# Vector products for the first two modulations: both weight tiles of a step loaded together, matmuls dealt to four column groups in turn

## The chip, the cores and the metric

The kernel runs on one core of a Trainium2 chip. The metric is device time in microseconds (us) of one launch. Before the change it is 1731.16 us, the median of three runs (1730.43 to 1734.97). A difference is given against that median.

## The reference, cut to what matters

One layer of a diffusion backbone, for 256 latent and 256 context tokens of width 2048, all in float32:

```python
mod_x = jnp.split(jax.nn.silu(c) @ w_ada + b_ada, 6, axis=-1)            # 6 rows of 2048
mod_c = jnp.split(jax.nn.silu(c_ctx)[None] @ w_ada + b_ada, 6, axis=-1)
qr, kr, vr, gr, cq, ckv, kpe = split_projection(modulate(x, mod_x[0], mod_x[1]) @ w_in)
qr_c, kr_c, vr_c, gr_c, cq_c, ckv_c, kpe_c = split_projection(modulate(ctx, mod_c[0], mod_c[1]) @ w_in)
# retention heads and latent attention heads over both streams, then
mix = jnp.concatenate([ret, from_heads(att)], -1) @ w_o
h = layer_norm(DEEPNORM_ALPHA * x + mod_x[2][:, None] * mix, ln1_w, ln1_b)
y = moe(modulate(h, mod_x[3], mod_x[4]))                                 # 32 gated experts, top 2
x_out = layer_norm(DEEPNORM_ALPHA * h + mod_x[5][:, None] * y, ln2_w, ln2_b)
```

`modulate` normalises a token and applies one shift (modulation 0) and one scale (modulation 1). These two have to be there before a block of `w_in` can be used; the change is in how they are computed.

## The kernel before

**Input projection in stages.** The first fifth of the kernel multiplies the modulated tokens with `w_in` (2048 x 4928). The contraction is cut into 16 blocks of 128, and these into six stages of 1, 1, 2, 4, 4 and 4 blocks (`STAGES`). Each stage goes over ten column blocks (nine of 512, one of 320). Five of them are for latent tokens alone, and five for context tokens too; all stages but the last take the five latent ones first. A stage loads its part of `w_in` in chunks of up to 1 MB: 3, 3, 5, 10, 10 and 10 chunks. A chunk is split into two float32r parts, a cast on ACT (L262, `whi`) and a subtraction on DVE (L263, `wlo`), and each product is three matmuls (L583 to L585): 24 for a full chunk of a latent column block, 48 with context. DVE adds the result to what earlier stages left (L592). A chunk's matmuls wait for `whi` and then for `wlo`.

**Vector products for modulations 0 and 1.** While stage s runs, shift and scale for the blocks of stage s+1 are made (`gemv_plan`, L503 to L530); those of the first stage are made at the start. Their weights (`ada01`) are tiles of 1 MB: one tile holds 16, 8 or 4 of the 16 contraction blocks, for one of the two modulations, at a width of 128, 256 or 512 columns. One matmul per contraction block k (L515) has 32 columns of weights (`csil`, two of them used) and writes 32 rows of one PSUM bank, the column group g = 2*m + k%2: tiles of shift use groups 0 and 1, tiles of scale groups 2 and 3. So a stage has 2, 4 or 8 tiles, each a `piece` of its own, in the order shift, scale, shift, scale. A last piece copies the bank on ACT (L521), adds up the groups with small matmuls (L524) and adds the bias on DVE (L526, `modc`). `modc` is used when tokens are transposed and modulated for the next stage (`xhat`; transposes L168, ACT L545, DVE L547). Rows of the trace count two records to a matmul of L515.

**Where the pieces stand.** After the matmuls of chunk ci the loop issues n = ceil(left / max(1, chunks - 2 - ci)) pieces. With ten chunks and nine pieces that is 2 after chunk 0 and 1 after each of the chunks 1 to 7.

**Loads.** All tiles of `w_in` and `ada01` go through `stream` (L141) into one pool `st` of four 1 MB buffers, on SP's queue, which issues in order and waits where the next buffer is not free. Rows of `w_ada` for modulations 2 to 5 (`ada25`) go through the same queue into a pool `sa` of two buffers; DVE uses them (L239, two instructions to a tile), some of them during the stages. The scheduler of the framework sets the order on each engine when the program is built; the queues then run in that order.

**After the projection** come retention, latent attention, output projection with the first norm, the router, the experts (382 loads of 1 MB) and the second norm.

## Time and profile before

| | us |
|---|---|
| median of three runs | 1731.16 |
| the three runs | 1730.43, 1731.16, 1734.97 |
| span of the profiled execution | 1728.5 |
| TensorE (PE) busy in it | 1595.0 (92%) |
| VectorE (DVE) busy | 860.4 (50%) |
| ScalarE (ACT) busy | 381.5 (22%) |

The profile gives no time for the profiled execution besides its span; the median of the runs lies 2.7 us above the span. PE is TensorE's matmuls, PEld its weight loads, SP the engine on whose queue the loads stand. In a row, `out<-in` are the names of the tiles that an instruction writes and reads (pG is the PSUM bank of the vector products, pA a bank of the projection, pT one for transposes), and what stands in square brackets is the engine's idle time before it, with what ended it.

### The profile page before, as it was taken

Reading aid. Unit: us, or ns where it says so; the run is one execution under the profiler, and the core shown is the slowest. Engines: PE = TensorE matmul, PEld = TensorE weight load, DVE = VectorE, ACT = ScalarE, POOL = GpSimd, SP = SyncE. Lnnn points to the kernel's source line nnn. Section 1 sums busy time; section 2 is a strip of 40 time slices with the busy share of each in tenths; the row PEclk is TensorE's granted clock in tenths of the full one; section 3 lists DMA queues with packets and bytes.
Section 4 is the critical chain, followed back from the end, with each engine's and each line's share of the span. In section 5 each row is a group of like instructions: output and inputs, shape, how many; then the busy total and the mean of one; then the engine's idle time right before and its main releaser. Section 6 shows DMA issues by size and latency. Waiting matters only on the chain. (4 is left out here: it accounts for less than half of the span.)

```text
span 1728.5 us, 21531 instructions
## 1 busy us (share of the span) xinstructions
PE 1595.0 (92%) x8730; PEld 958.4 (55%) x8730; DVE 860.4 (50%) x1563; ACT 381.5 (22%) x710; POOL 115.2 (7%) x94
## 2 busy tenths in 40 slices
PE   5999999987889899599999979999999999999995
PEld 4667686866868777344454434554444454444442
DVE  6877685798798777622331321332323233232306
ACT  3323232334665433410100000110010011001010
POOL 1000000074322100200000000000000000000001
PEclk8999999999999999799999999999999999999998
DMA  7787777756554589798999998999999999999981
GB/s 317 282 330 284 304 305 282 271 206 225 187 195 168 227 301 360 297 368 347 417 419 417 417 376 332 409 420 419 415 418 420 416 418 419 418 416 417 419 303 49
DMA packets 81591, 579.36 MB, mean 335 GB/s; under 512 B 9360, under 2 KB 9808, under 8 KB 11856
## 3 DMA queue, kind: packets, MB, share of 16 engines
q1 hardware_dynamic: 81360, 577.91, 83.8%
q8 instruction: 70, 1.15, 0.3%
q14 instruction: 33, 0.27, 0.0%
q0 software_dynamic: 128, 0.03, 0.0%
HBM read 575.81 MB, written 2.10 MB: 334 GB/s over the span
## 5 line engine op out<-in xcount | busy, mean ns | idle before, releaser
L1013 PE MATMUL pA<-st,xg 128*64 128x512 f32 x2032 | 447.5, 593 | 0.1
L1013 PEld LDWEIGHTS pA<-st,xg 128*64 128x64 f32 x2032 | 144.3, 137 | 273.0 <-issue 255.1
L1031 PE MATMUL pA<-st,hT 128*64 128x256 f32 x2048 | 238.5, 383 | 4.6 <-ACT hT L1022 4.6
L1017 DVE TENSOR_TENSOR hid<-pA,hid 128x256 f32<-128x256 f32 x32 | 13.6, 425 | 420.1 <-ACT hid L1016 420.1
L1031 PEld LDWEIGHTS pA<-st,hT 128*64 128x64 f32 x2048 | 140.0, 137 | 109.1 <-issue 26.9
L584 PE MATMUL pA<-wlo,xhi 128*128 128x512 f32 (+1 forms) x480 | 188.1, 392 | 10.3 <-DVE wlo L263 10.2
L583 PE MATMUL pA<-whi,xhi 128*128 128x512 f32 (+1 forms) x480 | 185.4, 394 | 3.4 <-ACT whi L262 3.3
L262 ACT CAST whi<-st 128x1024 fp32r<-128x1024 f32 (+3 forms) x130 | 124.7, 962 | 287.0 <-PE pA L585 175.0
L1035 DVE TENSOR_TENSOR Dm<-pA,ada_acc 64x256 f32<-64x256 f32 x256 | 108.1, 422 | 160.7 <-PE pA L1031 158.3
L585 PE MATMUL pA<-whi,xlo 128*128 128x512 f32 (+1 forms) x480 | 185.8, 387 | 0.0
L239 DVE SCALAR_TENSOR_TENSOR ada_acc<-st,c,ada_acc 128x1024 f32<-128x1024 f32 x128 | 176.8, 1401 | 11.2 <-DMA st<-in_ada_dram 11.0
L263 DVE TENSOR_TENSOR wlo<-st,whi 128x1024 fp32r<-128x1024 f32 (+2 forms) x122 | 134.7, 1112 | 56.0 <-ACT whi L262 55.4
L988 PEld LDWEIGHTS pT<-oh,nn 128*128 128x128 f32 x1024 | 125.6, 196 | 38.8 <-issue 38.0
L988 PE MATMUL pT<-oh,nn 128*128 128x128 f32 x1024 | 138.5, 286 | 7.1 <-PEq L1046 5.5
L994 ACT ACTIVATE xg<-pT,modt 128x128 f32<-128x128 f32 x128 | 58.4, 458 | 332.9 <-DVE xg L997 328.7
L1041 PE MATMUL pA<-Dm,sT 128*128 128x512 f32 x256 | 121.2, 596 | 4.9 <-DVE Dm L1035 4.9
L1016 ACT ACTIVATE hid<-pA 128x256 f32<-128x256 f32 x32 | 12.3, 384 | 497.2 <-PE pA L1013 497.2
L1042 DVE TENSOR_TENSOR h<-pA,h 128x512 f32<-128x512 f32 x128 | 88.3, 690 | 57.2 <-PE pA L1041 57.2
L583 PEld LDWEIGHTS pA<-whi,xhi 128*128 128x128 f32 x480 | 90.5, 191 | 37.6 <-ACT whi L262 17.9
L584 PEld LDWEIGHTS pA<-wlo,xhi 128*128 128x128 f32 x480 | 91.8, 191 | 32.2 <-DVE wlo L263 14.5
L585 PEld LDWEIGHTS pA<-whi,xlo 128*128 128x128 f32 x480 | 92.0, 192 | 16.3
L997 DVE TENSOR_SCALAR xg<-pT,modt 128x128 f32<-128x128 f32 x128 | 52.1, 408 | 50.8 <-PE pT L988 23.1
(342 smaller groups left out, 1462.2 us busy)
## 6 DMA issues: line engine op xcount, KB each, us to landing
st<-in_wexp_dram SPq DMA_DIRECT2D x382, 1024.0 KB, 12.3
st<-in_ada_dram SPq DMA_DIRECT2D x96, 1024.0 KB, 6.8
st<-in_win_dram SPq DMA_DIRECT2D x35, 1024.0 KB, 6.8
st<-in_wo_dram SPq DMA_DIRECT2D x16, 1024.0 KB, 5.0
st<-in_wuq_dram SPq DMA_DIRECT2D x3, 1024.0 KB, 4.8
xn<-in_x_dram SPq DMA_DIRECT2D x2, 1024.0 KB, 6.5
xn<-in_ctx_dram SPq DMA_DIRECT2D x2, 1024.0 KB, 17.0
st<-in_wukv_dram SPq DMA_DIRECT2D x2, 1024.0 KB, 5.0
```

Of the source, the lines that this page charges most:

```text
L239: V.scalar_tensor_tensor(accs[m][:, sl], w[:, sl], c2[:, k, 0:1], accs[m][:, sl], op0=OP.mult, op1=OP.add)
L262: A.copy(hi, src)
L263: (eng or V).tensor_tensor(lo, src, hi, op=OP.subtract)
L583: T.matmul(banks[t][:, :wd], xh[:, sl], hi[:, kk, :wd], start=fst, stop=False)
L584: T.matmul(banks[t][:, :wd], xh[:, sl], lo[:, kk, :wd], start=False, stop=False)
L585: T.matmul(banks[t][:, :wd], xl[:, sl], hi[:, kk, :wd], start=False, stop=lst)
L988: T.matmul(p[:, 128 * j:128 * j + width], nn[:, t, 128 * (k4 + j):128 * (k4 + j) + 128], oh[:, t, :width], start=(t == 0), stop=(t == 1))
L1013: T.matmul(pg[64 * cg:64 * cg + 64], xg[:, k, c0:c0 + 64], c[:, kk, 512 * cg:512 * cg + 512], start=(k == 0), stop=(k == KB - 1))
L1031: T.matmul(pd[64 * cg:64 * cg + 64, :256], hT[:, f % 2, 64 * (f // 2):64 * (f // 2) + 64], c[:, f, 256 * cg:256 * cg + 256], start=(f == 0 ...
L1035: V.tensor_tensor(Dm[rows, sl], pd[64 * cg:64 * cg + 64, :256], mod5[rows, sl], op=OP.mult)
L1041: T.matmul(p, sT[:K, t, :], Dm[:K, sl], start=True, stop=True)
L1042: V.tensor_tensor(h[:, t, sl], p, h[:, t, sl], op=OP.add)
```

## The change

A piece takes both tiles of a step j, of shift and of scale. They are loaded one directly behind the other, and the matmuls go over both: for each contraction block shift, then scale, so that the groups come in the order 0, 2, 1, 3. What is added into which group in which order is as before. A stage has 1, 2 or 4 such pieces and the last one, so with ten chunks and five pieces one comes after each of the chunks 0 to 3 and the last one after chunk 4. (The diff also takes out comments; from here on L515 is L517, L521 is L523, L524 is L526, L526 is L528, and L583 to L592 are one more.)

```diff
-        def piece(j, m):
+        def piece(j):
             def go():
                 if "p" not in box:
                     box["p"] = bank("G", 1)
                 p = box["p"]
-                c = stream(dram2(a["ada01"], base + (m * nch + j) * 128 * per * w, 128, per * w), per * w)
+                c = [stream(dram2(a["ada01"], base + (m * nch + j) * 128 * per * w, 128, per * w), per * w)
+                     for m in range(2)]
                 for kk in range(per):
                     k = j * per + kk
-                    g = 2 * m + (k % 2)
-                    T.matmul(p[32 * g:32 * g + 32, :w], csil[:, k], c[:, kk * w:kk * w + w],
-                             start=(k < 2), stop=(k >= KB - 2))
+                    for m in range(2):
+                        g = 2 * m + (k % 2)
+                        T.matmul(p[32 * g:32 * g + 32, :w], csil[:, k], c[m][:, kk * w:kk * w + w],
+                                 start=(k < 2), stop=(k >= KB - 2))
             return go
...
         for j in range(nch):
-            pieces.append(piece(j, 0))
-            pieces.append(piece(j, 1))
+            pieces.append(piece(j))
         return pieces + [last]
```

PE at the start, where shift and scale of the first block are made. `st_140` is the tile of shift, `xn_113` the normalised tokens. Before:

```order
L515 MATMUL pG_139<-st_140,csil_105 32x128 x16
L515 MATMUL pG_139<-st_158,csil_105 32x128 x16
L168 MATMUL pT_183<-ct_69,xn_113 128x128 x2
L524 MATMUL pG_178<-ct_69,row_176 128x4
L583 MATMUL pA_217<-whi_219,xhi_181 128x512
```

After (`st_142` is the tile of scale):

```order
L517 MATMUL pG_139<-st_140,csil_105 32x128
L168 MATMUL pT_183<-ct_69,xn_113 128x128 x2
L517 MATMUL pG_139<-st_142,csil_105 32x128
L517 MATMUL pG_139<-st_140,csil_105 32x128
L517 MATMUL pG_139<-st_142,csil_105 32x128
```

The two transposes of tokens stood behind all 32 products and now stand behind the first of them.

SP's queue in the stage of blocks 8 to 11, at its first chunks. `in_win` is `w_in`, `in_ada01` the weights of the vector products, `in_ada25` those of the later modulations. Before:

```order
L141 DMA st_1901<-in_win_dram 128x2048
L141 DMA st_2262<-in_ada25_dram 128x2048
L141 DMA st_1939<-in_ada01_dram 128x2048
L141 DMA st_2340<-in_ada25_dram 128x2048
L141 DMA st_1949<-in_win_dram 128x2048
L141 DMA st_1987<-in_ada01_dram 128x2048
L141 DMA st_1997<-in_win_dram 128x2048
L141 DMA st_2035<-in_ada01_dram 128x2048
L141 DMA st_2045<-in_win_dram 128x2048
L141 DMA st_2083<-in_ada01_dram 128x2048
```

After:

```order
L141 DMA st_1901<-in_win_dram 128x2048
L141 DMA st_2475<-in_ada25_dram 128x2048
L141 DMA st_1939<-in_ada01_dram 128x2048
L141 DMA st_2545<-in_ada25_dram 128x2048
L141 DMA st_1941<-in_ada01_dram 128x2048
L141 DMA st_1955<-in_win_dram 128x2048
L141 DMA st_1993<-in_ada01_dram 128x2048
L141 DMA st_1995<-in_ada01_dram 128x2048
L141 DMA st_2009<-in_win_dram 128x2048
L141 DMA st_2047<-in_ada01_dram 128x2048
L141 DMA st_2049<-in_ada01_dram 128x2048
L141 DMA st_2063<-in_win_dram 128x2048
```

Tiles of `w_in` and `ada01` alternated one to one; now two of `ada01` stand between two of `w_in`, and the four buffers of `st` go round in that order.

DVE at the end of the vector products in the stage of blocks 4 to 7. `modc` is the finished shift and scale, `wlo` the second part of the next tiles of `w_in`. Before:

```order
L592 TENSOR_TENSOR lv_95<-pA_1567,lv_95 128x512
L592 TENSOR_TENSOR cv_98<-pA_1568,cv_98 128x512
L592 TENSOR_TENSOR cv_98<-pA_1569,cv_98 128x512
L526 TENSOR_TENSOR modc_138<-pG_1632,bsel_108 128x16
L263 TENSOR_TENSOR wlo_1741<-st_1706,whi_1740 128x1024
L547 TENSOR_TENSOR xlo_1643<-xf_1647,xhi_1642 128x256
```

After:

```order
L263 TENSOR_TENSOR wlo_1333<-st_1328,whi_1332 128x1024
L263 TENSOR_TENSOR wlo_1349<-st_1328,whi_1348 128x1024
L592 TENSOR_TENSOR lg_96<-pA_1330,lg_96 128x512
L592 TENSOR_TENSOR lg_96<-pA_1331,lg_96 128x512
L528 TENSOR_TENSOR modc_138<-pG_1422,bsel_108 128x16
L263 TENSOR_TENSOR wlo_1387<-st_1382,whi_1386 128x1024
L263 TENSOR_TENSOR wlo_1403<-st_1382,whi_1402 128x1024
```

`modc` stood behind chunk 7, a context column block, and ahead of the split of the next chunk but one; it now stands behind chunk 3 (`lg`, a latent column block) and ahead of both splits of chunk 4 (`st_1382`), the chunk that PE takes next.

## Rows read from the trace of the kernel before

**Rows 1.** The head of the profile's page: the span, and the busy time of the engines.

```profile
span 1728.5 us, 21531 instructions
PE 1595.0 (92%) x8730; PEld 958.4 (55%) x8730; DVE 860.4 (50%) x1563; ACT 381.5 (22%) x710; POOL 115.2 (7%) x94
```

**Rows 2.** Busy time of the engines by stretch: the stretch, its length, busy time and instructions of PE, PEld, DVE, ACT and POOL, PE's granted clock as a share of full speed, the DMA engines' share, GB/s. The first two stretches are the stages of blocks 4 to 7 and 8 to 11, the others the last stage with retention and what follows it.

```profile
122.50:220.20 97.70, 97.70 (x446) 70.22 (x446) 67.53 (x82) 27.08 (x37) 0.00 (x0) 1.00 0.79 306
220.20:319.00 98.80, 98.80 (x482) 73.62 (x482) 68.12 (x81) 27.11 (x38) 2.30 (x2) 1.00 0.76 294
319.00:440.00 121.00, 106.17 (x512) 88.34 (x512) 108.03 (x169) 52.89 (x105) 53.08 (x49) 0.93 0.62 221
440.00:560.00 120.00, 108.24 (x624) 90.54 (x623) 104.02 (x195) 75.35 (x162) 32.46 (x18) 0.98 0.52 183
```

**Rows 3.** PE in order of time at three places of the 512 wide products: start in us, duration in us, engine, line, operation, tiles, shapes, records. The places are one matmul alone, one tile alone, and two tiles (of two pieces) with nothing between them.

```profile
146.42 1.05 PE L515 MATMUL pG<-st,csil 128*32 128x512 f32 x2
147.40 0.50 PE L584 MATMUL pA<-wlo,xhi 128*128 128x512 f32 x1
...
193.49 1.91 PE L515 MATMUL pG<-st,csil 128*32 128x512 f32 x8
195.33 0.50 PE L583 MATMUL pA<-whi,xhi 128*128 128x512 f32 x1
...
244.68 0.39 PE L584 MATMUL pA<-wlo,xhi 128*128 128x512 f32 x1
244.91 0.39 PE L585 MATMUL pA<-whi,xlo 128*128 128x512 f32 x1
245.23 1.94 PE L515 MATMUL pG<-st,csil 128*32 128x512 f32 x16
247.09 0.50 PE L583 MATMUL pA<-whi,xhi 128*128 128x512 f32 x1
247.43 0.40 PE L584 MATMUL pA<-wlo,xhi 128*128 128x512 f32 x1
```

**Rows 4.** The same view at the products 128 wide (first two rows) and 256 wide (next two), and at a run of three tiles 512 wide with the row behind it.

```profile
37.75 1.65 PE L515 MATMUL pG<-st,csil 128*32 128x128 f32 x22
...
47.26 1.97 PE L515 MATMUL pG<-st,csil 128*32 128x128 f32 x40
...
58.15 0.62 PE L515 MATMUL pG<-st,csil 128*32 128x256 f32 x2
...
65.06 1.92 PE L515 MATMUL pG<-st,csil 128*32 128x256 f32 x16
...
105.20 3.63 PE L515 MATMUL pG<-st,csil 128*32 128x512 f32 x24
109.58 0.73 PE L583 MATMUL pA<-whi,xhi 128*128 128x512 f32 x2 [0.75 <-ACT whi L262]
```

**Rows 5.** SP's queue from the second to the fifth stage: what a load waited for before it was issued, us in total, times, the longest in us.

```profile
SPq L141 <- PE pG L515: 146.4, 25, 10.9
```

**Rows 6.** Three loads issued one behind the other into an idle queue at 247.18, 247.60 and 248.07 us: tile, queue, number, size, us from issue to landing.

```profile
st<-in_win_dram SPq DMA_DIRECT2D x1, 1024.0 KB, 4.9
...
st<-in_ada_dram SPq DMA_DIRECT2D x1, 1024.0 KB, 7.0
...
st<-in_win_dram SPq DMA_DIRECT2D x1, 1024.0 KB, 9.0
```

**Rows 7.** Groups of instructions in 122.5 to 325 us, shapes kept apart: line, engine, operation, tiles, shapes, number, busy time in us, mean ns of one, idle time of the engine before them.

```profile
L239 DVE SCALAR_TENSOR_TENSOR ada_acc<-st,c,ada_acc 128x1024 f32<-128x1024 f32 x39 | 48.3, 1277 | 0.0
L263 DVE TENSOR_TENSOR wlo<-st,whi 128x1024 fp32r<-128x1024 f32 x37 | 44.8, 1221 | 25.6 <-ACT whi L262 25.3
L262 ACT CAST whi<-st 128x1024 fp32r<-128x1024 f32 x37 | 38.5, 1047 | 125.9 <-PE pA L585 109.8 <-DMA st<-in_win_dram 16.1
L521 ACT COPY row<-pG 128x512 f32<-128x512 f32 x2 | 1.2, 588 | 1.6 <-PE pG L515 1.6
```

**Rows 8.** PE and DVE in order of time at the end of the vector products in the stage of blocks 4 to 7.

```profile
219.38 0.95 PE L524 MATMUL pG<-ct,row 128*128 128x4 f32 x8
220.18 0.49 PE L583 MATMUL pA<-whi,xhi 128*128 128x512 f32 x1
220.36 0.17 DVE L526 TENSOR_TENSOR modc<-pG,bsel 128x16 f32<-128x16 f32 x1
220.65 1.23 DVE L263 TENSOR_TENSOR wlo<-st,whi 128x1024 fp32r<-128x1024 f32 x1
```

**Rows 9.** PE in order of time at the start of the kernel, and DVE in the same stretch.

```profile
12.52 5.72 PE L515 MATMUL pG<-st,csil 128*32 128x128 f32 x64 [12.52 <-DMA st<-in_ada_dram]
18.17 0.44 PE L168 MATMUL pT<-ct,xn 128*128 128x128 f32 x2
...
14.95 1.34 DVE L199 TENSOR_SCALAR xn<-xn,bnm,bnr 128x2048 f32<-128x2048 f32 x1
...
22.79 0.69 DVE L590 COPY lq<-pA 128x512 f32<-128x512 f32 x1 [0.71 <-PE pA L585]
23.39 2.46 DVE L194 BATCH_NORM_STATS2 bns<-xn 128x6 f32<-128x512 f32 x4
```

**Rows 10.** Two more stretches by engine, as in rows 2, in the first stage.

```profile
20.80:24.40 3.60, 3.50 (x8) 2.50 (x9) 2.89 (x5) 0.80 (x2) 0.00 (x0) 0.53 1.01 419
...
31.30:38.00 6.70, 5.79 (x17) 3.49 (x19) 4.66 (x9) 2.98 (x7) 0.00 (x0) 0.50 0.71 273
```

## The prediction

> **What bounds the kernel now.** I read the page's head first [rows 1]: PE is busy 92% of the span. Then the busy time by stretch [rows 2]: in the two stages of blocks 4 to 7 and 8 to 11 PE has no gap at all (97.70 of 97.70 us and 98.80 of 98.80), at a granted clock of 1.00 (2.4 GHz), while DVE is busy 69% of the time and the loads use 0.76 to 0.79 of the DMA engines. So a microsecond of vector products that goes shortens the projection by one, as long as no load or split becomes late; in the last stage and behind it DVE is nearly as full as PE (108.03 of 121 us, 104.02 of 120). Next I read PE in order of time at the vector products [rows 3, 4], to see what they cost in each form; then what SP's queue waits for [rows 5] and how long a load takes [rows 6], since the change doubles what a step needs; last the start [rows 9, 10], where PE waits anyway.
>
> The span is 1728.5 us and the median 2.7 us more; differences are worked out in the span and put on the median.
>
> **What the products save.** Taken from the start of one row to the start of the next [rows 3]: a matmul alone takes 147.40 - 146.42 = 0.98 us, four of one tile (two groups, in turn) 195.33 - 193.49 = 1.84 us, and eight of two tiles whose pieces stand side by side 247.09 - 245.23 = 1.86 us. Groups 0, 1 and then 2, 3 already run beside each other there, without the matmuls dealt in turn. So the new order gives nothing where two tiles already stood together; the gain is that all tiles now come in twos. The order of PE tells where each stands. A matmul that the scheduler puts alone in front still costs 0.98.
>
> - 512 wide, during blocks 2 and 3: before 0.98 + 0.98 + 1.85 + 1.84 + 4.38 (three tiles in a row, 109.58 - 105.20 in [rows 4]) + 1.87 = 11.9; now 0.98 + 1.85 + 1.87 and 3.72 for two pairs = 8.4. Saved 3.5.
> - During blocks 4 to 7: before 0.98 + 1.86 + 6 x 1.84 = 13.9; now 0.98 + 1.86 + 0.98 + 3 x 1.86 = 9.4. Saved 4.5. Three fewer changes between the two shapes: around the products at 245.23 the spacing of the projection's matmuls grows from 0.23 to 0.32 ahead and 0.34 behind [rows 3], so 0.2 each, 0.6. Together 5.1.
> - During blocks 8 to 11: before 1.86 + 6 x 1.84 = 12.9, now 1.86 + 0.98 + 1.86 + 2 x 1.86 = 8.4; with three changes of shape 5.1.
> - 256 wide: two tiles side by side 16 records in 1.85 (65.06), short blocks of one to two matmuls 0.55 (58.15) [rows 4]. Before ten blocks, 9.0 us with seven changes of shape more inside them, 10.3; now six short ones, one long and three such changes, 5.7. Saved 4.6.
> - 128 wide: two groups take 1.65 us for 22 records, 75 ns each [rows 4]; four 37.5. The 62 records of 37.75 and 47.26 cost 3.6 and then 62 x 0.0375 = 2.3. Saved 1.3.
>
> Sum 19.6. The pair does 8 x 0.98 = 7.84 us of lone matmuls in 1.86, 4.2 times as fast [rows 3]; I go by that. The Trainium skill speaks against it: "TensorE: Matmul & The Clock Gate", Part 3 (Packing small matmuls), measured 3.07 times for four packed, not four; the row disagrees.
>
> **What the loads cost.** SP waited 146.4 us for buffers that the products still held [rows 5]; before, that was hidden. The buffers of `st` go round: W0 a0 a0' W1, then a1 a1' W2 a2. a1' and W2 take the buffers of a0 and a0' and are issued when pair 0's products end; before, one tile of `ada01` stood between two of `w_in`, and each load had two steps to land. Loads issued one behind the other land 4.9, 7.0 and 9.0 us after their issue [rows 6]. From the end of pair 0 PE has 24 matmuls (5.71 us, 25 spacings of 0.23) and pair 1 (1.86), 7.57 us. W2, second in the queue and issued 0.4 later, lands at 7.4, its first part is cast in 1.05 [rows 7], so PE waits about 0.9. The whole stretch before the last pair has one such step in the 256 wide stage (1.0), 1.5 in the first 512 wide one (W1 there is behind pair 0 too), two in the next (1.6) and one in the last (0.8). Sum 4.9. Ends: 0 (the queue is not idle, but W2 may come before the gap that I assume), and with W2 third in the queue 9.0 + 0.4 + 1.05 - 7.57 = 2.9, and with `wlo` behind it (1.22) up to 3.5 a step.
>
> **What the end of the products costs.** Before, the small matmuls stood among those of a chunk already split (219.38, 220.18), and `modc` (220.36) had a split behind it that PE did not need at once [rows 8]. Now the last pair and the last piece stand behind one another on PE, and both splits of chunk 4, the next on PE, stand behind `modc` on DVE. After the last pair: copy of the bank 0.59 and its hand-over, 0.75; small matmuls 0.81 (220.18 - 219.38); `modc` 0.17; `wlo` 1.22: 2.95. Of that 0.81 was paid before, and some 0.2 runs beside whi's matmuls, so 1.9 a stage, for three stages 5.7. Ends: 0.7 (only the copy is waited for) and 2.2 each. No other work covers it: chunk 4 is next on PE, and the 24 matmuls before it are done.
>
> **The start.** 31 of the 32 products now stand behind two transposes that need the second token tile, ready at 14.95 + 1.34 = 16.29 [rows 9]. Before they ran from 12.52 to 18.17, 89 ns a record. Now 16.29 + 0.44 and 62 records at half of that, 2.8, end at 19.5, 1.3 later. On DVE one more copy (0.69) goes ahead of the context's statistics (23.39): 0.7. PE now stands idle up to 16.3, and I expect the stretches at 0.5 of the clock (1.2 GHz), which come after PE had worked little (20.80 to 24.40 and 31.30 to 38.00, [rows 10]), to take in some of the products; bound 0 and 2.8 (the products at half speed), I take 1.4. Sum 3.4; ends 2.0 and 62 x 0.089 + 0.44 + 16.29 - 18.17 + 0.7 = 4.8.
>
> Behind the projection nothing is moved that bears on the sum: the same tiles of `ada25` (two instructions of 1.28, [rows 7]) come before the end of the third 512 wide stage.
>
> **Sum.** -19.6 + 4.9 + 5.7 + 3.4 = -5.6: span 1722.9, median 1731.2 - 5.6 = 1725.6.
>
> **Rivals.**
> - B, the loads come in time. For it: the DMA engines have a quarter free in these stages [rows 2]. Against: the buffers set when a load starts, not the bandwidth. -19.6 + 5.7 + 3.4 = -10.5, 1720.7; with the split's wait at its lower end (3 x 0.7) 1717.
> - C, four groups give less in the new order than in the one place read: 1.86 was measured with the groups in the order 0, 1, 0, 1 and then 2, 3, 2, 3, not dealt in turn. A pair then lies between 1.86 and 2 x 1.84 = 3.68; at 2.5, 0.64 more for 12 pairs, it is 7.7: -5.6 + 7.7, 1733.3. Against: groups that are free of each other have no reason to care for the order. By the 3.07 of the Trainium skill's page "TensorE: Matmul & The Clock Gate", Part 3, a pair would take 7.84 / 3.07 = 2.55, near that value.
> - D, slower: W tiles land third. Its place is SP's queue: tiles of `ada25` stand between those of a step in the stage of blocks 8 to 11, and in a chunk of latent columns a step asks for 3 or 4 MB in 7.57 us where the third load lands at 9.0 [rows 6]. Then a step waits 3.5, five steps 17.5, and -19.6 + 17.5 + 5.7 + 3.4 = +7.0, 1738.2. It decides from 2.1 a step (19.6 - 5.7 - 3.4 = 10.5 in five steps). For it: nothing but the four buffers runs ahead. Against: two loads fit in a step, and before the `ada25` tiles came in the same places without a wait.
> - E, the gain isn't passed on: DVE, at 108.03 of 121 us in the last stage [rows 2], starts earlier but ends when it did, since SP's queue and its two `ada25` buffers feed it. 1731.
>
> **Chances.** The forecast (waits as summed, -5.6) 0.50, its own range 1720 to 1731; B 0.20, C 0.04, D 0.15, E 0.11. A measurement of this kernel can tell about 0.3%, 5.2 us, from no change. The forecast lies 0.4 beyond that bound: of its 0.50 I give 0.28 to faster, 0.21 to the same, 0.01 to slower; B gives 0.19 and 0.01; C 0.03 to the same and 0.01 to slower; D 0.04 to the same (where a step waits 2.1 to 2.9) and 0.11 to slower; E 0.01, 0.09 and 0.01. Faster 0.48, same 0.38, slower 0.14. The range of 8 in 10 leaves out the lower part of B and the upper half of D: 1715 to 1737.
>
> **What would show it.** Right: the pairs of eight 512 wide matmuls take 1.86 us each; PE has gaps of 0.8 to 1 us before `whi` of the third and fourth chunk of a stage, released by ACT, with the load landed about a microsecond before; a gap near 2 us behind the last pair, released by the copy and then by `wlo`; the first product of the projection starts 1 to 3 us after 20.80; the stage of blocks 4 to 7 is 1 to 2 us shorter than 97.7. Wrong on the loads: no gaps before `whi` (B), or gaps of 3 us and more with W third in the queue (D). Wrong on the groups: pairs of 2.5 us. Wrong on the passing on: the projection ends earlier by the sum, but the experts' loads begin no earlier (E).

## The result and the profile after

The changed kernel takes 1755.47 us (median of four runs, 1753.58 to 1755.84), the kernel before 1733.07 in the same comparison: a ratio of 1.0122, 95% interval 1.0105 to 1.0140. It is slower by 22 us, where 1725.6 us was forecast and the range ended at 1737. The spans of the two profiled executions are 1753.3 and 1728.5 us, 24.8 apart.

The head of the page after, which answers to [rows 1]:

```profile
span 1753.3 us, 21525 instructions
PE 1596.0 (91%) x8730; PEld 963.2 (55%) x8730; DVE 856.8 (49%) x1563; ACT 381.1 (22%) x710; POOL 111.8 (6%) x94
```

PE is busy as long as before, but that is not the same work. The matmuls of the vector products alone, over the first 420 us, before and after (busy time and records of PE and PEld, then PE's granted clock, the DMA engines' share, GB/s):

```profile
0.00:420.00 420.00, 58.98 (x384) 19.69 (x384) 0.97 0.74 284
```

```profile
0.00:420.00 420.00, 42.18 (x384) 12.90 (x384) 0.95 0.75 285
```

They are busy 16.8 us less. That PE's total doesn't fall goes with the clock: the mean granted clock of the span is 0.967 after and 0.979 before, and a matmul at half clock counts as busy for longer. PE's idle time grew by 23.8 us, from 133.5 to 157.3.

To see where, I took the same instruction in both traces as a mark: DVE's last addition of the 320 wide column block in each stage of the projection, the cast of the seventh `kn` tile (latent attention) and the last cast but one of `w_o` (output projection). That block is the last of a stage, except in the last stage, where it is the seventh of ten; so the stretch called latent attention begins with the last three chunks of the projection. The stretches of [rows 2] were cut elsewhere, at the end of a stage's vector products. Lengths from mark to mark in us, for the two kernels and for the experiments below:

| | start, block 0 | block 1 | 2, 3 | 4 to 7 | 8 to 11 | last stage, retention | latent attention | output projection |
|---|---|---|---|---|---|---|---|---|
| before | 54.05 | 36.04 | 53.41 | 96.74 | 98.82 | 126.71 | 87.17 | 127.68 |
| after | 55.46 | 32.93 | 61.01 | 97.10 | 102.38 | 132.86 | 91.75 | 129.04 |
| nodeal | 49.78 | 36.03 | 59.77 | 97.13 | 98.96 | 131.83 | 91.24 | 127.50 |
| oneload | 56.08 | 32.84 | 49.37 | 91.18 | 96.71 | 134.27 | 91.35 | 127.70 |
| startb | 49.16 | 33.47 | 61.99 | 97.24 | 100.01 | 131.46 | 92.17 | 127.60 |
| spread | 55.83 | 32.87 | 61.12 | 91.72 | 95.33 | 131.97 | 91.60 | 127.30 |
| eb2 | 54.36 | 32.79 | 61.07 | 96.88 | 98.47 | 132.42 | 91.41 | 127.53 |
| wahead | 53.98 | 32.95 | 61.80 | 99.16 | 100.64 | 133.40 | 91.97 | 127.48 |
| spread2eb | 50.27 | 32.99 | 57.67 | 90.98 | 95.33 | 131.22 | 93.74 | 128.00 |
| beb2 | 51.04 | 36.02 | 53.54 | 96.74 | 100.46 | 127.44 | 88.16 | 127.70 |
| eb4 | 55.57 | 33.01 | 61.34 | 97.28 | 102.93 | 131.09 | 92.49 | 127.54 |
| mix | 49.32 | 33.08 | 55.27 | 90.94 | 96.89 | 128.40 | 91.79 | 129.16 |
| mixav2 | 51.83 | 33.19 | 54.78 | 103.12 | 103.53 | 120.78 | 91.57 | 127.72 |
| aq | 53.73 | 32.78 | 60.59 | 97.02 | 98.37 | 129.85 | 95.04 | 128.84 |
| mixq | 52.30 | 32.91 | 54.84 | 90.93 | 95.29 | 130.82 | 96.33 | 129.26 |
| bq | 50.81 | 36.03 | 53.41 | 96.72 | 100.42 | 127.30 | 90.81 | 125.26 |
| a_noada | 57.00 | 32.93 | 61.99 | 96.29 | 98.39 | 107.22 | 79.19 | 125.63 |
| b_noada | 49.83 | 33.02 | 57.51 | 95.71 | 102.05 | 105.47 | 79.09 | 127.99 |

Some of these kernels run the same instructions in the same order up to a mark, and show how far one profile can be trusted. The start takes 50.8 to 54.1 in three profiles of before's order (before, beb2, bq) and 53.7 to 55.6 in four of after's (after, eb2, eb4, aq); the stage of blocks 8 to 11 takes 98.8 to 100.5 and 98.4 to 102.9. The other stages up to block 11 repeat within a microsecond. The last stage does not: with the same order on every engine it takes 132.9 in after and 129.9 in aq, and 128.4 in mix and 130.8 in mixq.

By the means of these three and four profiles the projection up to block 11 is 8.1 us longer after: +2.8, -3.2, +7.6, +0.3, +0.6. In the two profiled executions the last stage is 6.2 longer (4.4 by the means of before with bq and after with aq), latent attention 4.6, the output projection 1.4, and all that follows 2.9. The last two are near what profiles of one and the same code differ by.

**The five-chunk stage.** PE after, at the products made during blocks 2 and 3 (answers to the last row but one of [rows 4]):

```profile
100.31 0.73 PE L584 MATMUL pA<-whi,xhi 128*128 128x512 f32 x2 [1.73 <-ACT whi L262]
101.26 1.17 PE L584 MATMUL pA<-whi,xhi 128*128 128x512 f32 x2 [0.21 <-ACT whi L262]
...
108.08 4.61 PE L517 MATMUL pG<-st,csil 128*32 128x512 f32 x32
113.40 1.06 PE L526 MATMUL pG<-ct,row 128*128 128x4 f32 x8 [0.72 <-ACT row L523]
115.32 1.14 PE L168 MATMUL pT<-ct,xn 128*128 128x128 f32 x4 [0.86 <-ACT xf L546]
117.02 1.22 PE L584 MATMUL pA<-whi,xhi 128*128 128x512 f32 x2 [0.55 <-ACT whi L262]
```

From 108.08 on the two last pairs, the last piece and the transposes run with nothing of the projection among them: 8.9 us until the next matmul with `w_in` at 117.02. SP's queue there shows why (start, duration until the last of the group is issued, how many):

```profile
92.19 0.37 SPq L141 DMA_DIRECT2D st<-in_win_dram  x1
92.65 10.36 SPq L141 DMA_DIRECT2D st<-in_ada_dram  x4
110.04 3.49 SPq L141 DMA_DIRECT2D st<-in_win_dram  x4
```

A view prints `ada01` and `ada25` both as `in_ada`; the four of the second row are `ada01`. In this stage the loop puts two pairs after chunk 0 and two after chunk 1. The four `ada01` tiles of two pairs fill the four buffers. Behind chunk 1 the next tile of `w_in` is issued only at 110.04, when the first of the two pairs is done; it lands 4.8 later, and its cast makes PE wait to 117.02. The two pairs after chunk 0 delay the tile issued at 92.19 in the same way, and PE waits 1.73 for its cast (100.31).

**The clock.** The same three stretches before and after (columns as in [rows 2]), before first:

```profile
86.00:94.00 8.00, 8.00 (x40) 3.87 (x39) 7.74 (x13) 2.94 (x5) 0.00 (x0) 1.00 0.50 189
100.00:106.00 6.00, 6.00 (x32) 4.32 (x34) 3.52 (x5) 0.00 (x0) 0.00 (x0) 1.00 0.95 358
114.00:122.00 8.00, 8.00 (x46) 5.31 (x45) 5.15 (x7) 2.68 (x3) 0.00 (x0) 1.00 0.88 360
```

```profile
86.00:94.00 8.00, 7.22 (x35) 3.56 (x34) 7.03 (x11) 1.58 (x2) 0.00 (x0) 1.00 0.54 197
100.00:106.00 6.00, 5.47 (x16) 4.05 (x17) 3.15 (x4) 1.21 (x2) 0.00 (x0) 0.72 0.97 386
114.00:122.00 8.00, 6.58 (x21) 4.68 (x21) 4.27 (x8) 5.35 (x10) 0.00 (x0) 0.57 0.94 393
```

In before's profile the clock is 1.00 in every 2 us from 86 to 340. After, it falls to 0.5 (1.2 GHz) behind the wait that ends at 100.31, again behind those at 112 to 117, and for a few us near 170, 264 and 290. PE counts as busy in such a stretch and does half the work. Not every fall has a wait before it: near 264 PE had not waited for anything since 188, and in beb2 and bq, which run before's order, the clock falls near 256 with PE busy all the time. This is beb2:

```profile
256.00:259.40 3.40, 3.40 (x11) 2.73 (x10) 0.00 (x0) 0.00 (x0) 1.83 (x2) 0.50 0.91 321
```

What such a stretch costs depends on what sets the pace. In eb2 and aq, with after's order, the clock stays at 1.00 behind the wait that ends at 100.31 after, and the whole stage of blocks 2 and 3 is no shorter (after, eb2, aq; the clock is the last column but two):

```profile
88.39:149.40 61.01, 56.24 (x264) 39.57 (x264) 40.15 (x57) 17.37 (x28) 0.00 (x0) 0.92 0.74 282
```

```profile
87.14:148.22 61.08, 54.06 (x264) 37.60 (x264) 40.16 (x57) 17.38 (x28) 0.00 (x0) 0.97 0.76 286
```

```profile
86.51:147.10 60.59, 53.94 (x263) 37.59 (x264) 40.14 (x56) 17.20 (x28) 0.00 (x0) 0.97 0.78 288
```

PE's busy time falls by 2 us there and its waits grow by as much (in eb2 it waits 1.45 at 110.05 for an `ada01` tile to land): the loads set the pace. In the stage of blocks 8 to 11 it is otherwise. There the clock stays at 1.00 in eb2 and aq, which take 98.5 and 98.4 us; it is 0.95 in after and eb4, which take 102.4 and 102.9.

**The two ten-chunk stages.** The waits in the stage of blocks 4 to 7 after, at a late tile of `w_in` and at the end of the products:

```profile
167.36 0.73 PE L584 MATMUL pA<-whi,xhi 128*128 128x512 f32 x2 [1.09 <-ACT whi L262]
168.62 0.50 PE L585 MATMUL pA<-wlo,xhi 128*128 128x512 f32 x1 [0.53 <-DVE wlo L263]
...
185.66 1.06 PE L526 MATMUL pG<-ct,row 128*128 128x4 f32 x8 [0.73 <-ACT row L523]
186.61 0.73 PE L584 MATMUL pA<-whi,xhi 128*128 128x512 f32 x2
188.12 0.50 PE L585 MATMUL pA<-wlo,xhi 128*128 128x512 f32 x1 [0.78 <-DVE wlo L263]
```

That is 1.6 for the loads and 1.5 for the end. The stage of blocks 8 to 11 has the same four waits (0.94, 0.53, 0.73 and 0.78).

**The products themselves** came out as forecast: two tiles 512 wide take 177.30 - 175.45 = 1.85 us, and the 62 records 128 wide now 50.71 - 48.83 = 1.88, less than the 2.3 us of the prediction.

```profile
48.83 1.95 PE L517 MATMUL pG<-st,csil 128*32 128x128 f32 x62
50.71 0.50 PE L584 MATMUL pA<-whi,xhi 128*128 128x512 f32 x1
...
175.45 1.92 PE L517 MATMUL pG<-st,csil 128*32 128x512 f32 x16
177.30 0.74 PE L584 MATMUL pA<-whi,xhi 128*128 128x512 f32 x2
```

### The profile page after: what moved, and what is told of

The parts are those of the page before. It is cut to its first block, busy times and chain, and to the rows that moved or that the text cites. A ratio compares the mean times of both kernels' runs of the same rounds, so it can differ in the third digit from the quotient of the medians.

```text
span 1753.3 us, 21525 instructions
## 1 busy us (share of the span) xinstructions
PE 1596.0 (91%) x8730; PEld 963.2 (55%) x8730; DVE 856.8 (49%) x1563; ACT 381.1 (22%) x710; POOL 111.8 (6%) x94
## 5 line engine op out<-in xcount | busy, mean ns | idle before, releaser
L584 PE MATMUL pA<-whi,xhi 128*128 128x512 f32 (+1 forms) x480 | 185.7, 399 | 17.0 <-ACT whi L262 16.8
L1036 DVE TENSOR_TENSOR Dm<-pA,ada_acc 64x256 f32<-64x256 f32 x256 | 108.1, 422 | 160.6 <-PE pA L1032 158.3
L239 DVE SCALAR_TENSOR_TENSOR ada_acc<-st,c,ada_acc 128x1024 f32<-128x1024 f32 x128 | 176.6, 1400 | 14.6 <-DMA st<-in_ada_dram 14.5
L586 PEld LDWEIGHTS pA<-whi,xlo 128*128 128x128 f32 x480 | 93.2, 194 | 16.8 <-DVE xlo L548 0.2
```

The costliest lines, as they stand in the source:

```text
L239: V.scalar_tensor_tensor(accs[m][:, sl], w[:, sl], c2[:, k, 0:1], accs[m][:, sl], op0=OP.mult, op1=OP.add)
L584: T.matmul(banks[t][:, :wd], xh[:, sl], hi[:, kk, :wd], start=fst, stop=False)
L586: T.matmul(banks[t][:, :wd], xl[:, sl], hi[:, kk, :wd], start=False, stop=lst)
L1036: V.tensor_tensor(Dm[rows, sl], pd[64 * cg:64 * cg + 64, :256], mod5[rows, sl], op=OP.mult)
```

## The experiments

Theories first: Q, tiles of `w_in` come late because `ada01` tiles stand before them in a queue with four buffers, and the clock falls after each wait; F, the dealt groups themselves cost; S, the start; and for what lies behind block 11, where no line was changed: O, the engines' order, which the scheduler works out anew for the whole program; P, DVE with its `ada25` work. Each kernel's time is one run unless an interval is given.

**nodeal.** The pairs without the dealing: shift's tile, then scale's.

```diff
-                for kk in range(per):
-                    k = j * per + kk
-                    for m in range(2):
+                for m in range(2):
+                    for kk in range(per):
+                        k = j * per + kk
```

> As the changed kernel, but a pair's eight matmuls run over the tile of shift first and then over that of scale, not dealt in turn. Marks are the end of the stage of blocks 8 to 11 (the last context column block added by DVE): 339.1 us before, 348.9 after. Theory Q (the tiles of w_in come late behind two ada01 tiles, and PE's clock falls after each wait): the order of the matmuls means nothing, a pair of 512 wide takes 1.9 us here too, and the mark lies at 347 to 351. Rival F (dealing to four groups itself costs): the pairs are quicker or the waits go, and the mark lies at 343 or below.

1742.9 us. The mark lies at 341.7, so by the bar set F wins. But the bar tells little: after's own order gives 342.5 to 350.1 (after, eb2, eb4, aq). By stage F does not win: the stages of blocks 2 to 7 are nearly as after (59.8, 97.1). The gain is at the start (49.8 against 55.5), where the products now run in before's order, and the stage of block 1 loses the saving again (36.0 against 32.9). There the scheduler scatters the small products into the same ten blocks as before, and only dealt ones find all four groups; at 512 wide a pair takes 1.87 us (171.63 to 173.50) undealt too.

**oneload.** A pair loads one tile and uses it twice.

```diff
-                     for m in range(2)]
+                     for m in range(1 if si else 2)]
+                c = (c + c)[:2]
```

> As the changed kernel, but from the second stage on a pair loads the tile of shift alone and uses it for scale too (the scale is wrong; 15 loads of 1 MB are left out). The same matmuls in the same places. Theory Q: with one ada01 tile to a step the next tile of w_in comes in time, the waits of the stage of blocks 2 and 3 (about 8 us) and of the two after it go, the granted clock is 1.00 from 122 to 319 us, and the end of the stage of blocks 8 to 11 lies at 328 to 334 (339.1 before, 348.9 after). Rival F (the four groups, or the end of the products behind modc, cost): the mark stays at 345 or above.

1732.2 us. The stages of blocks 2 to 11 take 49.4, 91.2 and 96.7, at a clock of 1.00 and with no gap in the first two (49.40 of 49.40 us busy, 91.18 of 91.20); in the third the clock is at 0.50 from 279.4 to 286.2, which theory Q had not expected. The mark lies at 326.2, below the 328 to 334 expected. So the saving is there, 4.0 and 5.6 us against before in the first two stages (3.5 and 5.1 forecast; 1.3 of the 4.0 were gaps before), and in the changed kernel the second load takes it and more. F falls.

**startb.** The start alone as before (a piece is told which tiles to take).

```diff
         for j in range(nch):
-            pieces.append(piece(j))
+            if si == 0:
+                pieces.append(piece(j, (0,)))
+                pieces.append(piece(j, (1,)))
+            else:
+                pieces.append(piece(j))
```

> As the changed kernel, but at the start the tiles of shift and scale are taken one after the other as before. Theory Q: only the start moves: the first cast of w_in at 20.1 as before (21.9 after), and the end of the stage of blocks 8 to 11 1 to 2 us earlier than after, 347 to 348. Rival S (the start delays the loads of the context and shifts the whole queue): more than 4 us of the 9.8 go.

1746.0 us. The first stage ends 6.3 us earlier than after, and the mark lies at 341.9, 7.0 earlier: by the bar set rival S, against the expectation. Against all four profiles of after's order (342.5 to 350.1) it is 0.6 to 8.3, so the size is not settled. PE at the start, after and then in this run:

```profile
12.38 0.60 PE L517 MATMUL pG<-st,csil 128*32 128x128 f32 x2 [12.38 <-DMA st<-in_ada_dram]
13.40 0.48 PE L168 MATMUL pT<-ct,xn 128*128 128x128 f32 x1 [0.42 <-DVE xn L199]
16.21 0.48 PE L168 MATMUL pT<-ct,xn 128*128 128x128 f32 x1 [2.33 <-DVE xn L199]
16.62 3.30 PE L517 MATMUL pG<-st,csil 128*32 128x128 f32 x62
20.32 0.39 PE L526 MATMUL pG<-ct,row 128*128 128x4 f32 x2 [0.41 <-ACT row L523]
```

```profile
12.29 4.75 PE L517 MATMUL pG<-st,csil 128*32 128x128 f32 x64 [12.29 <-DMA st<-in_ada_dram]
16.97 0.44 PE L168 MATMUL pT<-ct,xn 128*128 128x128 f32 x2
17.41 0.39 PE L526 MATMUL pG<-ct,row 128*128 128x4 f32 x2
19.60 0.50 PE L588 MATMUL pA<-whi,xhi 128*128 128x512 f32 x1 [1.81 <-ACT whi L262]
```

The transposes ahead of the products hold PE to 16.62, as forecast from [rows 9], and the first matmul with `w_in` comes at 22.51 against 19.60: 2.9. The rest goes with the clock, which in this run is 1.00 throughout the first stage, and 0.63 from 31.3 to 38 us after.

**spread.** Pairs after chunks 0, 2, 4 and 6 in the ten-chunk stages.

```diff
+            if nchunk == 10 and todo:
+                n = 1 if ci in (0, 2, 4, 6, 7) else 0
```

> As the changed kernel, but in the ten-chunk stages the pairs come after chunks 0, 2, 4 and 6 and the last piece after chunk 7. Theory Q: each pair's loads have two steps again, so the stages of blocks 4 to 7 and 8 to 11 take 93 to 95 us each at a clock of 1.00 (96.7 and 98.8 before, 97.1 and 102.4 after), while the stage of blocks 2 and 3 stays at 60 to 62 (53.4 before, 61.0 after). Rival F: those stages stay at 97 or more. Theory O for what comes behind (the scheduler's order on ACT in the last stage, not the lateness): the stretch from the end of the stage of blocks 8 to 11 to the last split of the output projection, 341.6 before and 353.7 after, follows the order of ACT there; rival P (lateness carried on by loads): it falls back to about 342 as the lateness goes.

1740.3 us. 91.7 and 95.3 in the two stages, 61.1 in the one that was not spread: theory Q, the first even below its 93 to 95, and 5.0 and 3.5 us under before. What follows block 11 stays long (132.0 and 91.6) though this kernel is 2 us ahead of before at that mark, so lateness is not handed on.

**eb2, eb4.** The second decay table in two and in four buffers.

```diff
-        Eb = rt.tile([128, 384], F32, name="Eb", bufs=1)
+        Eb = rt.tile([128, 384], F32, name="Eb", bufs=2)
```

In the last stage PE waited 8.9 us for a cast on ACT after, and ACT for POOL:

```profile
390.82 0.80 PE L584 MATMUL pA<-whi,xhi 128*128 128x512 f32 x1 [8.91 <-ACT whi L262]
392.07 0.80 PE L585 MATMUL pA<-wlo,xhi 128*128 128x512 f32 x1 [0.46 <-DVE wlo L263]
```

```profile
388.42 0.61 ACT L350 ACTIVATE Eb<-rfb,r_lg 128x384 f32<-128x384 f32 x1 [8.61 <-POOL Dt L351]
388.94 0.89 ACT L355 ACTIVATE xq<-rfb,r_lg 128x256 f32<-128x256 f32 x2
389.74 1.03 ACT L262 CAST whi<-st 128x1024 fp32r<-128x1024 f32 x1
```

> As the changed kernel, but the second decay table of a retention head (Eb, L350 on ACT, used by POOL at L351) has two buffers in place of one. Up to the end of the stage of blocks 8 to 11 nothing is changed (mark at 348 to 350). Theory O (in the last stage the scheduler now puts the second head's Eb on ACT ahead of the cast of a w_in tile, and that Eb waits for POOL): PE's wait of 8.9 us for that cast goes, and the stretch from that mark to the last addition of the 320 wide column block falls from 132.9 to 125 to 128 us (126.7 before). Rival P (POOL and DVE are simply full there, so another wait takes its place): it stays at 131 or more.

> As the changed kernel, with Eb in four buffers (in the run with two, the third head's Eb stood ahead of the next cast and waited for POOL in the same way). Theory O: with no Eb waiting, ACT's casts of the last stage come in time, and the stretch from the end of the stage of blocks 8 to 11 to the last addition of the 320 wide block falls from 132 to 125 to 128 us. Rival P (DVE, with three more ada25 instructions of 1.3 to 1.8 us in the stretch than before, 39 against 36, and POOL beside it are the bound): another wait of the same size takes its place and it stays at 131 or more.

1747.1 and 1753.9 us. The wait for the cast goes, and DVE takes its place: with four buffers PE has this row there,

```profile
387.89 0.80 PE L585 MATMUL pA<-wlo,xhi 128*128 128x512 f32 x1 [4.02 <-DVE wlo L263]
```

and the stretch is 132.4 and 131.1, within the 129.9 to 132.9 of after's own order. The longest wait of a view was not the cause; O falls for ACT, P stands.

**wahead.** The next chunk's tile of `w_in` is loaded ahead of the pair's two.

```diff
+            if si >= 2 and n and ci + 1 < nchunk:
+                nw = sum(NBW[m] for m in chunks[ci + 1])
+                ahead[ci + 1] = stream(dram2(a["win"], off, 128, nk * nw), nk * nw)
             for f in todo[:n]:
```

> As the changed kernel, but from the third stage on the next chunk's tile of w_in is loaded ahead of a pair's two tiles, not behind them. Theory Q (the tile of w_in is late because it stands behind ada01 tiles in a queue of four buffers): the stages of blocks 2 and 3, 4 to 7 and 8 to 11 take 54 to 57, 92 to 95 and 95 to 98 us (61.0, 97.1 and 102.4 after). Rival L (a step simply asks for more than the loads bring, whatever the order): the waits move to the products, and the stages stay within 2 us of after.

1754.2 us; 61.8, 99.2 and 100.6: rival L. The order in the queue is not the point. I read it as three tiles a step in four buffers, whichever stands first: fewer tiles a step (oneload) and more steps (spread) help. A pool with more buffers was not run.

**spread2eb and beb2.** The first puts startb, spread and eb2 together, with one pair after each of the chunks 0 and 1, two after chunk 2 and the last piece after chunk 3 of the five-chunk stage; the second is before with eb2's line.

```diff
+            if nchunk == 5 and todo:
+                n = (1, 1, 2, 1, 0)[ci]
```

> The pairs and the dealt matmuls, with the start as before, the pairs after every second chunk in the ten-chunk stages, after chunks 0, 1, 2 (two) and 3 in the five-chunk stage, and Eb in two buffers. Theory Q with S and O: the stages take 49, 33, 52 to 56, 91 to 93 and 95 to 97, the last stage's stretch 125 to 128 as in the run with Eb alone, and the total is 1720 to 1729, 2 to 11 us below before. Rival: the stage of blocks 2 and 3 keeps its waits (62), and the total stays within 3 us of before or above it.

> The kernel before with Eb in two buffers, nothing else. Theory O: before, the cast stood ahead of the waiting Eb, so there is little to gain: the stretch from the end of the stage of blocks 8 to 11 to the last addition of the 320 wide block is 122 to 127 us (126.7), the total 1727 to 1734. Rival: Eb's single buffer cost before as well, 5 us or more, and the total falls below 1727.

1733.08 us, ratio 1.0010 (0.9995 to 1.0025), and 1732.14, ratio 0.9999 (0.9989 to 1.0009): no difference that can be measured in either. For the first the rival holds: 57.7 in the stage of blocks 2 and 3 where 52 to 56 was expected, 131.2 behind it where 125 to 128 was, and no gain in the total. It is 11.8 us ahead of before at the end of block 11 (327.2) and has given nearly all of it back by the end of latent attention (131.2 and 93.7). That left what lies behind as the question.

**mix and mixav2.** The start and the products of the five-chunk stage singly, the others in pairs, spread in the ten-chunk stages. mixav2 adds Eb's four buffers and moves `ada25` tiles forward in the program:

```diff
-ADA_V = [[0] * 10, [0] * 10, [0] * 5, [1] * 10, [1] * 10, [2] * 4 + [1] * 6]
+ADA_V = [[0] * 10, [0] * 10, [1] * 5, [1] * 5 + [2] * 5, [1] * 5 + [2] * 5, [1] * 10]
```

> Pairs dealt to four groups only where two steps lie between them: the start and the products made during the five-chunk stage are taken singly as before, those of the 128 and 256 wide stages in pairs, those of the two ten-chunk stages in pairs after chunks 0, 2, 4 and 6. Theory Q: stages of 49 to 51, 33, 53 to 54, 91 to 92 and 95 to 96, so the stage of blocks 8 to 11 ends at 321 to 326 us (339.1 before). The rest decides the total: if the stretches behind follow the engines' order, which is nearer to before's here (88 ada25 instructions on DVE up to the last addition against 94 after and 86 before), 126 to 129 and 87 to 89 and a total of 1715 to 1721; if pairs as such make them longer, 131 to 133 and 91 to 93 and 1723 to 1729.

> The run before this one, with Eb in four buffers, and with more of the ada25 tiles put into the stages of blocks 2 to 11 (5, 15 and 15 in place of 0, 10 and 10) and fewer into the last stage: 70 of DVE's 128 ada25 instructions stand ahead of the end of the stage of blocks 8 to 11 (50 before), 32 in the stretch behind (36 before, 39 after). If DVE's ada25 instructions bound that stretch (rival P), it falls to 124 to 128, for 7 fewer of 1.3 to 1.8 us than after; the stages of blocks 2 to 11 grow by 0 to 6 us in all, since their DVE has room (69% busy before) but their loads less. If not, it stays at 131. The total 1714 to 1728.

mix: 1729.78 us, ratio 0.9984 (0.9967 to 1.0001), the lowest median, and just not told from before; latent attention takes 91.8 where the better case was to bring 87 to 89. mixav2: 1735.83, ratio 1.0020 (1.0007 to 1.0034), above its 1714 to 1728. But its last stage is the shortest, 120.8. DVE's `ada25` instructions in that stretch, in before, after and mixav2:

```profile
L239 DVE SCALAR_TENSOR_TENSOR ada_acc<-st,c,ada_acc 128x1024 f32<-128x1024 f32 x36 | 52.4, 1466 | 4.3 <-DMA st<-in_ada_dram 4.2
```

```profile
L239 DVE SCALAR_TENSOR_TENSOR ada_acc<-st,c,ada_acc 128x1024 f32<-128x1024 f32 x39 | 56.1, 1464 | 3.1 <-DMA st<-in_ada_dram 3.1
```

```profile
L239 DVE SCALAR_TENSOR_TENSOR ada_acc<-st,c,ada_acc 128x1024 f32<-128x1024 f32 x32 | 46.5, 1465 | 2.8 <-DMA st<-in_ada_dram 2.8
```

Over all kernels above and below that keep this work, 32 instructions go with 120.8 us, 36 with 126.7 to 127.4, 38 with 128.4 and 130.8, and 39 with 129.9 to 133.4. oneload does not fit (37 and 134.3). In mixav2 the stages before paid more than that back: 103.1 and 103.5, where mix has 90.9 and 96.9. So the place of these tiles is a balance; that before has it about right is a guess from this one other place.

**aq, mixq and bq.** In latent attention, the transposes of the rotated queries behind the first products, on after, mix and before: the loop that fills `qa` is moved behind `up(0)` and takes its bank from the projection's.

```diff
-        for hp in range(0, 4, 2):
-            p = bankT()
...
         up(0)
+        for hp in range(0, 4, 2):
+            p = bankA()
```

> As the changed kernel, but in latent attention the transposes of the rotated queries stand behind the first heads' products (their PSUM tile is taken from the projection's banks, which come free only then). Up to there nothing changes. Theory O (the order on PE is the cause): the wait of 3 us for the rotated queries and the stretch at half clock go, and the stretch of latent attention falls from 91.8 to 86 to 88.5 us. Rival V (DVE, which is 83% busy there, is the bound): another wait for DVE takes its place, and it stays at 90 or more.

> The mixed version (pairs only in the stages with room) with the transposes of the rotated queries behind the first heads' products. Theory O: latent attention in 86 to 89 us (91.8 in the mixed version), the rest as there, a total 3 to 6 us under the mixed version's 1729.8: 1723 to 1727, faster than before. Rival V: 1728 to 1731.

> The kernel before with the same move of the transposes and nothing else. Before, PE waited 2.5 us at the place where latent attention begins and its clock stayed at 1.00, so by theory O little is to be had: 85 to 88 us there (87.2), total 1730 to 1734. If it falls by 3 us or more here too, the move helps whatever the pairs do, and the mixed version's gain is to be compared with this one.

aq 1749.1 us; mixq 1733.12, ratio 1.0002 (0.9986 to 1.0017); bq 1735.57, ratio 1.0019 (1.0004 to 1.0034). Latent attention becomes longer, not shorter (95.0, 96.3 and 90.8), in bq too, where 85 to 88 was expected: rival V. The wait moved to the split of `kv` on DVE (4.57 us in aq). Ahead of it on DVE after:

```profile
507.44 2.36 DVE L239 SCALAR_TENSOR_TENSOR ada_acc<-st,c,ada_acc 128x1024 f32<-128x1024 f32 x1
509.72 0.86 DVE L428 SCALAR_TENSOR_TENSOR mix<-pT,sm,mix 128x256 fp32r<-128x256 f32 x2
510.50 2.62 DVE L239 SCALAR_TENSOR_TENSOR ada_acc<-st,c,ada_acc 128x1024 f32<-128x1024 f32 x1
```

Before, one stood in this place, between the last addition (L592, at 489.28) and the rotation (L301):

```profile
494.24 1.27 DVE L239 SCALAR_TENSOR_TENSOR ada_acc<-st,c,ada_acc 128x1024 f32<-128x1024 f32 x1
495.44 0.86 DVE L428 SCALAR_TENSOR_TENSOR mix<-pT,sm,mix 128x256 fp32r<-128x256 f32 x2
496.22 0.40 DVE L301 TENSOR_TENSOR P<-PT,rot 128x256 f32<-128x256 f32 x1
```

After, two stand there, each at about twice its usual 1.28 (L593 at 503.32, the rotation at 513.83). That is only a part of the 4.6 us: from the mark to the rotation it is 30.5 before and 32.1 after, and the other 2.9 lie behind it. It is not a matter of number either: the stretch has 16 of these instructions before and 14 after.

**a_noada and b_noada.** Both kernels without `ada25`'s work: seven of eight loads and all large DVE instructions at L239 are left out. The kernels differ in their loads there too, so this can't tell the instructions from their loads.

```diff
-        w = stream(dram2(a["ada25"], ((m - 2) * KB + k) * 128 * D, 128, D), pool=sa)
-        for j in range(2):
...
+        if k % 8 == 0:
+            w = stream(dram2(a["ada25"], ((m - 2) * KB + k) * 128 * D, 128, D), pool=sa)
+            V.tensor_scalar(accs[m][:, 0:1], w[:, 0:1], c2[:, k, 0:1], None, op0=OP.mult)
```

> The changed kernel without the work for modulations 2 to 5 (their loads and DVE's instructions at L239 are left out but for one small one in eight, so these modulations are wrong); read up to the end of latent attention only. Theory P (DVE's ada25 instructions, in other places than before, make both stretches longer): the last stage's stretch and latent attention are within 1.5 us of the same marks in the kernel before without that work, and at least 8 us shorter than with it (132.9 and 91.8). Rival O (order on ACT, PE and POOL): they stay 4 us or more longer than there.

> The kernel before without the same work. Theory P: its last stage's stretch and latent attention equal those of the changed kernel without it, within 1.5 us each. Its stage of blocks 2 and 3 stays near 53 (that of the changed kernel near 61 if the waits there are the ada01 tiles', 55 or less if ada25's loads in the queue made them).

The last stage, the changed kernel first:

```profile
346.60:453.82 107.22, 102.08 (x544) 87.71 (x543) 59.71 (x149) 59.15 (x126) 46.42 (x58) 0.97 0.26 90
```

```profile
338.11:443.58 105.47, 100.53 (x544) 86.00 (x543) 59.59 (x150) 59.14 (x126) 45.96 (x58) 0.98 0.27 92
```

It takes 107.2 and 105.5, latent attention 79.2 and 79.1. Of the 6.2 us 1.8 are left, less than two profiles of one order differ by in this stage, and of the 4.6 only 0.1: theory P, a little short of its 1.5 in the first. So both differences need the `ada25` work. How it makes them is shown less well: DVE is busy 111.6 of 132.9 us after and 108.1 of 126.7 before, so it is not full, and with the work go its loads (the DMA engines' share falls from 0.61 to 0.26).

The stage of blocks 2 and 3 stays at 62.0 in the changed kernel, so the `ada25` loads do not make its waits. But in the kernel before it takes 57.5 where 53 was expected, with waits of 2.1 us for casts on ACT where before has 0.7; why is not known. So of the 7.6 us 4.5 are left here.

## Why the prediction was wrong

- **What bounds the kernel** was right for the projection and stopped too early: the row of DVE at 108 of 121 us [rows 2] stood in the argument and became rival E only.
- **What the products save**: right in the main. Where the loads are out of the way, 4.0 us for 3.5 (oneload, blocks 2 and 3), 5.6 and 5.0 for 5.1 (oneload and spread, blocks 4 to 7), and 2.1 and 3.5 for 5.1 (blocks 8 to 11, both with a stretch at half clock); block 1 net 3.1, for 4.6 less a wait of 1.0. Rival C fell: a pair takes 1.85. Its 2.55 took over a figure that the Trainium skill's page "TensorE: Matmul & The Clock Gate", Part 3 (Packing small matmuls), gives for four row tiles; these are column groups.
- **What the loads cost** is the first step that failed, as mis-sized: 1.5 for the stage of blocks 2 and 3, where the stage came out 11.6 longer than without the second load (61.0 and 49.4). I worked out a step with one pair, though my own sum of the products has two pairs together there (3.72): the plan puts two after chunk 0 and two after chunk 1, and their four tiles take all four buffers. In the stage of blocks 4 to 7 the size was right: waits of 1.09 and 0.53 for 1.6, though in one step and not in two. That stage is still 5.9 longer than without the second load (97.1 and 91.2); 3.1 of it are its waits, and a part is the clock (0.98 of full speed over the stage). The upper end of 3.5 a step, which rival D uses, does not follow from its terms: 2.9 and 1.22 are 4.1.
- **The clock** was a term of the start alone. In the stages the rows of before show 1.00, and I had nothing to read it from but [rows 10]. It was worth nothing in the stage of blocks 2 and 3, where loads set the pace, and about 4 us in the stage of blocks 8 to 11 (102.4 and 102.9 against 98.5 and 98.4 for one order).
- **The end of the products**: forecast 1.9 a stage, and nearly right. At the stage of blocks 4 to 7 PE waits 0.73 for the copy, goes on with `whi` already cast, and then waits 0.78 for `wlo`: 1.5, and the same in the stage of blocks 8 to 11.
- **The start**: forecast 3.4 less 1.3; measured 2.8 later by the means of the profiles, right in sum. Most of it is there when the first product of the projection starts, 22.5 to 23.0 us after against 20.1 to 20.8 before.
- **"Behind the projection nothing is moved that bears on the sum"** is the second step that failed: a term of nothing, measured as +6.2 (4.4 by means) and +4.6. The diff touches nothing there, but the scheduler's order of `ada25` on DVE changed with the pairs: 55 in place of 50 of 128 instructions by the end of block 11, then 39 in place of 36 in the last stage, and 20 in place of 26 behind latent attention. I had compared the number of tiles up to the third stage, by the program's numbers, and not the order on DVE: at the mark of the last stage it has done 94 of them after and 86 before.
- **Rivals**: D named the right place (SP's queue) and sign, with a size per step that no run bears out. E had the right engine and the wrong sign: DVE did not keep the gain, its work added a loss.

Either step alone would have put the time above the range. Where -5.6 us was forecast, the projection up to block 11 came out 8.1 longer by the means, which with nothing behind it gives about 1739 us; and what lies behind block 11 is 15 us longer in the two profiled executions, which on the forecast gives about 1741.

What stays open is why the scheduler takes these instructions so, how much of the loss behind block 11 is their number, their place or their loads, and what the 2.9 us behind the rotation in latent attention are.

## What to carry to other kernels

Merging two units of work that each need a load doubles what one step asks of the buffers: count tiles per step against the pool, at the step where the plan puts two units together, before counting what the merged instructions save. Where a scheduler orders the whole program, read its order on the engine that is fullest in later stages too, far from the edit, and count there what filler work moved in. Price a stretch at half clock only where PE sets the pace: where loads did, it cost nothing. And run the same order twice before reading a few microseconds out of one profile.

## What was not expected of the hardware

- PE's granted clock fell to 0.5 behind a wait of 1.73 us in a stream that was otherwise full (0.72 over 100 to 106 us after), but not behind the same wait in eb2 and aq; and it fell with PE busy throughout (beb2, 256 to 259.4 us), where before's profile of the same order shows 1.00.
- One and the same start ran 50.8 to 54.1 us in three profiles. In the slowest the clock was 0.50 at 31.3 to 38 us [rows 10], in the other two 1.00.
- DVE's 128x1024 instruction of 1.28 us took 2.36 and 2.62 in latent attention after, and one took 2.83 before (at 486.52), each beside a subtraction on POOL; it took 1.46 on average in the last stage, where POOL is at work too, and 1.28 in the stages before [rows 7].
